# Local attention's probabilities turned in 32x32 squares and put together in DRAM

## The chip, the cores and the metric

The kernel runs on one core of one Trainium2 chip. The metric is the device time of one execution in microseconds (us), the median of several runs. Four engines compute: TensorE (PE in the profile; its weight loads are PEld), VectorE (DVE), ScalarE (ACT) and GpSimd (POOL). SyncE (SP) issues the DMAs, one after the other from one queue. Each engine works through its instructions in the order in which they were written out, and waits where an operand isn't ready.

## The reference

The program is one layer of a decoder over 1024 tokens of width 1024, in float32. It has three branches (sparse attention, a convolution module, cross-attention to 256 memory tokens), which are merged by gates, and then a gated feed-forward network. The change lies in the sparse attention, which has 8 query heads in 2 groups of 4; the heads of a group share keys and values of width 64. Three kinds of attention are summed with a gate for each:

```
s_c = q . kc   -> p_c = softmax over the compressed blocks that have ended    -> o_c = p_c vc
s_s = q . ks   -> p_s = softmax over selected blocks of 64 keys, up to t      -> o_s = p_s vs
s_w = q . kw   -> p_w = softmax over the last 512 keys (local window)         -> o_w = p_w vw
o   = gate0 * o_c + gate1 * o_s + gate2 * o_w
```

With 1024 tokens there are 16 selectable blocks and 16 are taken, so "selected" is ordinary causal attention here. The local branch is causal attention over a window of 512 keys.

## The kernel before

Every matrix product keeps nearly full float32 accuracy by splitting operands into a high part (rounded to the type that PE multiplies fast) and the low remainder. The helper `split` (lines 130 to 132) does it: ScalarE writes the high part, VectorE (or GpSimd) the difference. All products go through `mm` (line 146), so most PE rows carry line 146.

**The attention's order of work.** The loop at lines 822 to 836 runs over 8 tiles of 128 query rows (`i`), 2 groups (`g`), and within a group over four units `(br, hp)`: the causal branch (`br` 1) for head pairs 0 and 1, and then the local branch (`br` 2) for head pairs 0 and 1. That makes 64 units. For a unit `scores` is written down; `values` of the same unit is written down `LAG` units later, just ahead of that later unit's `scores`. The compressed branch (`br` 0) has its scores in the first 64 columns of the causal branch's first product, and one `values` call for all four heads of a group.

**`scores`** (lines 726 to 777). At the first unit of a group the four heads' queries are scaled, turned by PE (line 735) and split. For each head the products of queries (high and low) with keys go into a PSUM bank of pool 0, up to 512 columns at a time. VectorE adds the mask and takes the running maximum in one instruction (line 769, written to `tiles`), ScalarE takes the exponential and its sum (line 773). `softmax_tail` (lines 691 to 699) takes the reciprocal of the sums on VectorE and scales the probabilities by reciprocal and gate on GpSimd. The probabilities stand with 128 query rows on the partitions and keys along the columns; the tile that holds two heads comes from the pool `slabs` or the pool `wsp` (`wslab`, 3 buffers), two and three times in five.

**`values`** (lines 779 to 820). To multiply with the values, the probabilities must have the keys on the partitions. For two key blocks and two heads at a time PE turns four 128x128 squares into one PSUM bank of pool 1 (line 803), `split` makes the two parts from there into a `t4` tile, and PE multiplies them with the stored values. The stationary operand holds the values' high and low parts side by side (64 columns each), so a block takes two products of 256 columns (two heads x 128 queries), one for each part of the probabilities. All three branches of a group add up in one bank `OB` (pool 2, one bank); the compressed branch starts it and the local branch's last product ends it. Then ScalarE and VectorE add the bank's two halves (lines 814 and 817), and SP stores the result to `od` in DRAM (line 820).

**Work that fills PE's gaps.** The products of the three merge gates (lines 839 to 860) are independent of the attention. They have the lowest priority; their weights come by DMA into `fst` and are split into the `fsl` tiles, they have one bank of their own (`pf`), ScalarE copies the result out (line 859) and SP stores it to `zd` (line 860). Beyond the first 12 of 24 column blocks, each may start only behind one of the attention's `anchors`, a list of (weight, instruction) pairs that `values` appends, so that they spread over the attention.

**What sets the order.** The program text gives each instruction a priority; a planner then simulates the engines and writes out one fixed order for each engine and for SP's queue, taking the first instruction in priority that its model believes ready, and hands out the buffers of each pool as they come free. `follow` adds an order between two instructions of one engine without a semaphore. PSUM has 8 banks: `cnt` (line 60) gives 3, 3 and 1 to pools 0, 1 and 2, and the last is `pf`'s. The same pools serve the later stages through `bank` and `anybank`; the last stage takes its eight banks by the list `pools` (line 1177).

## Time and profile before

| | |
|---|---|
| median of 3 runs | 1700.61 us (1700.05 to 1700.92) |
| the profiled execution | 1701.01 us, span 1699.3 us |
| PE busy | 1675.7 us (99%) |
| VectorE busy | 1074.8 us (63%) |
| ScalarE busy | 732.9 us (43%) |
| GpSimd busy | 517.7 us (30%) |
| moved by DMA | 211.81 MB |
| the attention's stretch | about 453 to 840 us of the span |

Times in the profile are us from the start of the span unless marked ns. A group row gives line, engine, operation, tiles (out<-in), shapes, count, then the busy time in us and the mean duration of one in ns, and the engine's idle time just ahead of it with what ended it. The busy time of a group counts overlapping matmuls once, so it is less than count times mean. A row of a timeline gives start, length and the merged run of instructions. Line numbers are the kernel's; a helper's line stands for all that call it.

### The profile page before, as it was taken

The page shows a single profiled execution, that of the slowest core. Times are in us where ns is not written, and L with a number is a line of the kernel's source. Part 1 is how long each engine was busy: PE and PEld are TensorE (multiplying, and loading weights), DVE is VectorE, ACT ScalarE, POOL GpSimd, SP SyncE. Part 2 cuts the span into 40 slices and gives each one's busy share as a digit, 9 for nine tenths or more (in the row PEclk, how much of TensorE's full clock was granted, in tenths as well). Part 3 has the DMA queues.
Part 4 walks back from the last instruction along what each step waited for, and adds up shares of the span by engine and source line. Part 5 has one row for each costly group of instructions (what it writes and reads, how often), then busy time and mean ns, then how long its engine had stood idle before and what let it go on. Part 6 is the DMA issues. An engine that isn't in the chain of part 4 may idle for free.

```text
span 1699.3 us, 23161 instructions
## 1 busy us (share of the span) xinstructions
PE 1675.7 (99%) x8424; PEld 1415.4 (83%) x8424; DVE 1074.8 (63%) x1890; ACT 732.9 (43%) x1376; POOL 517.7 (30%) x478
## 2 busy tenths in 40 slices
PE   7999999999999999999999999999999999999999
PEld 6887898888888889989888888788888888888887
DVE  6278888688446677777766626756445455466655
ACT  6311444342356667666655424433222222233332
POOL 0000002120145544534105501465656776310000
PEclk9999999999999999999999999999999999999999
DMA  8012444221122111111674323133233545793773
GB/s 282 34 40 87 140 135 129 99 94 63 50 76 69 51 51 38 48 38 48 225 252 137 113 86 121 64 119 118 88 112 114 167 147 170 280 392 129 230 231 124
DMA packets 176728, 211.81 MB, mean 125 GB/s; under 512 B 11284, under 2 KB 113988, under 8 KB 175590
## 3 DMA queue, kind: packets, MB, share of 16 engines
q1 hardware_dynamic: 176614, 210.34, 37.3%
q8 instruction: 66, 1.08, 0.3%
q14 instruction: 48, 0.39, 0.1%
HBM read 155.77 MB, written 54.53 MB: 124 GB/s over the span
## 4 chain that ended last, share of the span: by engine, by line
PE 93%; DVE 3%; DMA 2%; ACT 1%; issue 1%; POOL 0%; SPq 0%; ACTq 0%; DVEq 0%; POOLq 0%
PE ps L146 56%; PE pf L146 19%; PE ps L1251 11%; PE ps L803 3%; PE pf L1251 1%; DVE slab L132 1%; DMA slab<-in_x_dram 1%; DVE t L132 1%; PE ps L233 1%; DMA slab<-in_mem_dram 0%; PE ps L603 0%; PE ps L735 0%; PE ps L787 0%; DMA st<-in_w_in_dram 0%; ACT t L131 0%
## 5 line engine op out<-in xcount | busy, mean ns | idle before, releaser
L146 PE MATMUL ps<-slab,wsl 128*128 128x512 f32 (+1 forms) x1652 | 367.9, 381 | 1.9 <-DVE sm L140 0.8
L146 PEld LDWEIGHTS ps<-slab,wsl 128*128 128x128 f32 x1652 | 300.0, 188 | 63.4 <-issue 1.9
L146 PE MATMUL pf<-slab,fsl 128*128 128x512 f32 x1236 | 322.1, 399 | 1.5 <-ACT fz L859 1.5
L146 PEld LDWEIGHTS pf<-slab,fsl 128*128 128x128 f32 x1236 | 223.6, 188 | 43.5 <-ACT fz L859 2.6
L1147 DVE TENSOR_TENSOR t<-ps,t 128x512 f32<-128x512 f32 x130 | 88.8, 688 | 106.0 <-PE ps L146 104.6
L421 DVE SCALAR_TENSOR_TENSOR slab<-slab,cw 128x1023 f32<-128x1023 f32 (+14 forms) x120 | 152.2, 1268 | 2.1
L146 PE MATMUL ps<-slab,fsl 128*128 128x512 f32 x636 | 149.0, 391 | 1.6 <-DVE slab L132 1.6
L146 PEld LDWEIGHTS ps<-slab,fsl 128*128 128x128 f32 x636 | 119.2, 188 | 27.6 <-DVE slab L132 2.0
L146 PE MATMUL ps<-wsl,slab 128*128 128x512 f32 (+1 forms) x648 | 140.0, 360 | 0.1
L132 DVE TENSOR_TENSOR t<-ps,t 128x512 fp32r<-128x512 f32 (+2 forms) x192 | 117.8, 630 | 28.5 <-ACT t L131 27.2
L146 PE MATMUL ps<-t,slab 128*128 128x256 f32 (+1 forms) x672 | 127.7, 299 | 0.7 <-DVE t L132 0.7
L146 PEld LDWEIGHTS ps<-wsl,slab 128*128 128x128 f32 x648 | 108.1, 189 | 17.3 <-DVE slab L225 0.3
L146 PE MATMUL ps<-slab,slab 128*128 128x512 f32 x480 | 117.5, 396 | 1.3 <-ACT slab L224 0.9
L1251 PE MATMUL ps<-wsl 128*128 128x512 f32 x495 | 118.7, 389 | 0.0
L131 ACT CAST t<-ps 128x512 fp32r<-128x512 f32 (+2 forms) x192 | 98.9, 539 | 43.7 <-PE ps L803 20.0
L593 POOL TENSOR_SCALAR t<-t,sm 128x256 f32<-128x256 f32 x32 | 25.6, 816 | 291.2 <-DVE sm L589 261.5
L146 PEld LDWEIGHTS ps<-t,slab 128*128 128x128 f32 x672 | 102.9, 189 | 8.2 <-DVE t L132 1.2
L1251 PEld LDWEIGHTS ps<-wsl 128*128 128x128 f32 x495 | 92.9, 188 | 19.3
L146 PEld LDWEIGHTS ps<-slab,slab 128*128 128x128 f32 x480 | 90.8, 191 | 21.2 <-ACT slab L224 1.7
L131 ACT CAST wsl<-st 128x1024 fp32r<-128x1024 f32 x59 | 62.0, 1051 | 79.3 <-PE ps L146 42.4
L146 PE MATMUL ps<-slab,qt 128*128 128x384 f32 (+6 forms) x400 | 96.0, 337 | 0.0
L132 DVE TENSOR_TENSOR wsl<-st,wsl 128x1024 fp32r<-128x1024 f32 x58 | 74.6, 1287 | 31.9 <-ACT wsl L131 31.7
(249 smaller groups left out, 2722.3 us busy)
## 6 DMA issues: line engine op xcount, KB each, us to landing
t<-in_w_down_dram SPq DMA_DIRECT2D x70, 256.0 KB, 4.0
fst<-in_w_in_dram SPq DMA_DIRECT2D x24, 512.0 KB, 3.7
zd<-fz SPq DMA_DIRECT2D x48, 256.0 KB, 2.0
t<-zd SPq DMA_DIRECT2D x24, 512.0 KB, 4.4
st<-in_w_gate_dram SPq DMA_DIRECT2D x22, 512.0 KB, 4.1
st<-in_w_up_dram SPq DMA_DIRECT2D x22, 512.0 KB, 4.2
ad<-t SPq DMA_DIRECT2D x44, 256.0 KB, 2.6
st<-in_w_in_dram SPq DMA_DIRECT2D x20, 512.0 KB, 3.7
```

The costliest lines, as they stand in the source:

```text
L131: m = nc.scalar.copy(hi, src)
L132: return m, (eng or nc.vector).tensor_tensor(lo, src, hi.bitcast(F32), op=OP.subtract)
L146: m = nc.tensor.matmul(o, a, b, start=start, stop=stop)
L233: m = nc.tensor.transpose(b[:, kk, tt * P:(tt + 1) * P], js[tt][:, k * P:(k + 1) * P], ident)
L421: return nc.vector.scalar_tensor_tensor(acc[:, s:], u[:, :S - s], cw[:, ct, 30 - s:31 - s], acc[:, s:], op0=OP.mult, op1=OP.add)
L593: nc.gpsimd.tensor_scalar(pm[:, tt, h, :], pm[:, tt, h, :], rec[:, j:j + 1], 1.0, op0=OP.mult, op1=OP.mult)
L803: nc.tensor.transpose(b[:, j - j0, h, :], tiles[h][:, j * P:(j + 1) * P], ident)
L1147: nc.vector.tensor_tensor(o, a_, b_, op=OP.add)
L1251: nc.tensor.matmul(B[t], a_, b_, start=start and k == 0 and j == 0, stop=k == FH - 1 and j == 2, skip_group_check=True)
```

## The change

The local branch's probabilities are no longer turned by PE.

- VectorE turns each 32x32 square of them in place of PE (`turn_window`): for two heads at a time, so that the tile `T_` has, in each quarter of 32 partitions, a 32-key part of each of its columns' blocks on the partitions, and head and 32 queries along the columns. It is issued one unit later, behind the next unit's last maximum (`behind`). A fifth key block goes to the free end of the first head pair's tile.
- After the second head pair, SP stores each of the four quarters of partitions (`a`, 32 queries each) to a new DRAM tensor `wd`, by one DMA for up to four blocks and one for the fifth: pieces of 512 bytes. In `wd` the squares lie so that key blocks of 128 can be read with keys on the partitions and all four heads' queries along 512 columns.
- `window_values` loads two key blocks at a time from `wd` (512 KB), splits them in SBUF into `t4` tiles, and multiplies: two products of 512 columns (four heads) for a block. It runs in two parts, in the places of the two head pairs' `values`.
- The order within a group is turned round: the local branch's two units come first, then the causal branch's two. The local branch starts the bank `OB`, the causal branch ends it. There are two such banks (pool 2), and pool 1 has two in place of three; the last stage's list is changed to match. `LAG` is 6 in place of 4.
- The probabilities of the causal branch always come from `slabs`, those of the local branch from `wslab`; the counter `turn[0]`, which later stages use to alternate buffers, is no longer advanced in `scores`.
- One reciprocal instead of two serves the causal and compressed branches of a pair.

```diff
-WB, LAG, SPREAD = 6, 4, 97
+WB, LAG, SPREAD = 6, 6, 97
...
-    cnt = [3, 3, 1]
+    cnt = [3, 2, 2]
...
-        turn[0] += 1
-        pt = (wslab if turn[0] % 5 < 3 else slab)([2, S], F32)
-        tiles = [pt[:, h, :nb * P] for h in range(2)]
-        mn_, den = small(8), small(4)
+        if br == 1:
+            short = PC[(i, g)]
+            pt = slab([2, S], F32)
+            tiles = [pt[:, h, :nb * P] for h in range(2)]
+        else:
+            pt = wslab([2 * S], F32)
+            tiles = [pt[:, h * nb * P:(h + 1) * nb * P] for h in range(2)]
+        mn_, den, rec = small(8), small(4), small(4)
...
+        n = 4 if br == 1 else 2
+        nc.vector.reciprocal(rec[:, :n], den[:, :n])
...
+        for f_ in behind:
+            f_(peak.ins)
+        behind.clear()
+        if br == 2:
+            behind.append(lambda after: turn_window(i, g, hp, nb, pt, after))
         return tiles
+
+    def turn_window(i, g, hp, nb, pt, after):
+        full = min(nb, 4)
+        if hp == 0:
+            WT[(i, g)] = [(wslab([16, 4, 32], F32)[:, :4 * full], 0, full)]
+            if nb > 4:
+                t5 = pt[:, 2 * nb * P:2 * nb * P + 512].rearrange("p (n h q) -> p n h q", h=4, q=32)
+                WT[(i, g)].append((t5, 4, 1))
+        both = pt[:, :2 * nb * P].rearrange("p (h n k) -> p n h k", h=2, k=32)
+        for T_, j0, n in WT[(i, g)]:
+            follow(nc.vector.transpose(T_[:, :, 2 * hp:2 * hp + 2, :], both[:, 4 * j0:4 * (j0 + n)]), after,
+                   "turned behind the next maxima")
+        if hp == 1:
+            for T_, j0, n in WT[(i, g)]:
+                for a in range(4):
+                    nc.sync.dma_start(
+                        wd[2 * i + g, 4 * j0:4 * (j0 + n), :, a, :].rearrange("n k q -> k n q"),
+                        T_[32 * a:32 * a + 32].rearrange("p n h q -> p n (h q)"))
+
+    def window_values(i, g, part):
+        k0 = max(0, i - 4)
+        nb = i + 1 - k0
+        if part == 0:
+            OB[(i, g)] = bank([4, P], at=2)
+        o = OB[(i, g)].rearrange("p h (a q) -> p h a q", a=4)
+        pairs = list(range(0, nb, 2))
+        cut = (len(pairs) + 1) // 2
+        for j0 in (pairs[:cut] if part == 0 else pairs[cut:]):
+            n = min(2, nb - j0)
+            lo, hi = t4([2, 4, 4, 32], F32R), t4([2, 4, 4, 32], F32R)
+            nc.sync.dma_start(lo[:, :n].bitcast(F32).rearrange("p j a h q -> p j (a h q)"),
+                              wd[2 * i + g, 4 * j0:4 * (j0 + n)].rearrange("(j b) k a q -> (b k) j (a q)", b=4))
+            split(hi[:, :n], lo[:, :n], lo[:, :n].bitcast(F32))
+            for j in range(n):
+                for hl, t_ in enumerate((hi, lo)):
+                    m = mm(o, VSW[1][:, k0 + j0 + j, g, :], t_[:, j].rearrange("p a h q -> p h a q"),
+                           j0 == 0 and j == 0 and hl == 0, False)
+        if part == 0 or len(pairs) > 1:
+            anchors.append((WB + nb, m.ins))
...
-            for br, hp in ((1, 0), (1, 1), (2, 0), (2, 1)):
+            for br, hp in ((2, 0), (2, 1), (1, 0), (1, 1)):
...
-    pools = ([0, 0, 0, 2], [1, 1, 1, None])
+    pools = ([0, 0, 0, 2], [1, 1, 2, None])
```

More of the change, by code (lines that the diff above doesn't have):

```diff
@@ L689, in balanced, with softmax_tail @@
         return [n] if n <= 4 else [n - n // 2, n // 2]
-    def softmax_tail(i, g, br, h0, den, tiles):
-        n = len(tiles)
-        rec = small(n)
-        nc.vector.reciprocal(rec, den)
-        if br == 0 and i == 0:
-            nc.vector.tensor_scalar(rec, rec, rowok, None, op0=OP.mult)
-        for h in range(n):
+    def softmax_tail(i, g, br, h0, rec, tiles):
+        for h in range(2):
             c0 = (4 * g + h0 + h) * 3 + br
             nc.gpsimd.tensor_scalar(tiles[h], tiles[h], rec[:, h:h + 1], gsb[:, i, c0:c0 + 1], op0=OP.mult, op1=OP.mult)
-    QS, OB, QN, PC, anchors = {}, {}, {}, {}, []
+    QS, OB, QN, PC, WT, anchors, behind = {}, {}, {}, {}, {}, [], []
+    wd = drp.tile([2 * NT, 20, 32, 4, P], F32, tag="wd", name="wd")
     def load_q(i):
@@ L726, in scores @@
     def scores(i, g, br, hp):
-        if br == 1 and hp == 0:
+        if br == 2 and hp == 0:
             if g == 0 and i + 1 < NT:
@@ L768, in scores @@
                 acc = mn_[:, 3 * h + ci:3 * h + ci + 1]
-                nc.vector.tensor_tensor_reduce(tiles[h][:, o:o + n * P], b[:, lead:], m, op0=OP.add, op1=OP.min,
-                                               scale=-0.125, scalar=BIG if last is None else last, accum_out=acc)
+                peak = nc.vector.tensor_tensor_reduce(
+                    tiles[h][:, o:o + n * P], b[:, lead:], m, op0=OP.add, op1=OP.min, scale=-0.125,
+                    scalar=BIG if last is None else last, accum_out=acc)
                 last = acc
@@ L773, in scores @@
             nc.scalar.activation(tiles[h], tiles[h], AF.Exp, scale=-1.0, bias=last, accum_out=den[:, h:h + 1])
+        n = 4 if br == 1 else 2
+        nc.vector.reciprocal(rec[:, :n], den[:, :n])
         if br == 1:
-            softmax_tail(i, g, 0, 2 * hp, den[:, 2:4], short[2 * hp:2 * hp + 2])
-        softmax_tail(i, g, br, 2 * hp, den[:, 0:2], tiles)
-        return tiles
+            if i == 0:
+                nc.vector.tensor_scalar(rec[:, 2:4], rec[:, 2:4], rowok, None, op0=OP.mult)
+            softmax_tail(i, g, 0, 2 * hp, rec[:, 2:4], short[2 * hp:2 * hp + 2])
@@ new lines, in scores @@
+        softmax_tail(i, g, br, 2 * hp, rec[:, 0:2], tiles)
+        for f_ in behind:
[3 more added lines that the diff above has]
+            behind.append(lambda after: turn_window(i, g, hp, nb, pt, after))
+        return tiles
+    def turn_window(i, g, hp, nb, pt, after):
[15 more added lines that the diff above has]
+                        T_[32 * a:32 * a + 32].rearrange("p n h q -> p n (h q)"))
@@ L779, in values @@
     def values(u, tiles):
         i, g, br, hp = u
-        if br == 0:
-            OB[0] = bank([4, P], at=2)
-        o = OB[0]
+        if br == 2:
+            window_values(i, g, hp)
+            return
+        o = OB[(i, g)]
         if br == 0:
@@ L789, in values @@
             split(pt[:64], pt[64:], b[:64])
[L790 removed]
+            m = mm(o.rearrange("p h q -> p (h q)"), vcmp[:, g, :], pt.rearrange("p h q -> p (h q)"), False, False)
             anchors.append((3, m.ins))
             return
[L793 to L795 removed]
+        nb = i + 1
         oh = o[:, 2 * hp:2 * hp + 2, :].rearrange("p h q -> p (h q)")
@@ L808, in values @@
                 for hl in range(2):
-                    m = mm(oh, V[:, k0 + j, g, :], pt[:, hl, j - j0, :], False,
-                           br == 2 and hp == 1 and j == nb - 1 and hl == 1)
+                    m = mm(oh, VSW[0][:, j, g, :], pt[:, hl, j - j0, :], False,
+                           hp == 1 and j == nb - 1 and hl == 1)
         anchors.append((WB + nb, m.ins))
-        if br == 2 and hp == 1:
+        if hp == 1:
             bot = t2([2, 2, P], p=64)
```

7 lines of the change are left out of this document (2 added, 5 removed).

## The prediction

> **What bounds the kernel now.** I read the busy shares first, then the chain that ended last, then the stretch of the attention alone.
>
> ```profile
> PE 1675.7 (99%) x8424; PEld 1415.4 (83%) x8424; DVE 1074.8 (63%) x1890; ACT 732.9 (43%) x1376; POOL 517.7 (30%) x478
> PE 93%; DVE 3%; DMA 2%; ACT 1%; issue 1%; POOL 0%; SPq 0%; ACTq 0%; DVEq 0%; POOLq 0%
> PE ps L146 56%; PE pf L146 19%; PE ps L1251 11%; PE ps L803 3%; PE pf L1251 1%; DVE slab L132 1%; DMA slab<-in_x_dram 1%; DVE t L132 1%; PE ps L233 1%; DMA slab<-in_mem_dram 0%; PE ps L603 0%; PE ps L735 0%; PE ps L787 0%; DMA st<-in_w_in_dram 0%; ACT t L131 0%
> ```
>
> TensorE (PE) is the bound: busy 99%, and 93% of the chain. L803, the turning of probabilities that the change attacks, is 3% of the chain. So an instruction taken from PE is worth its own time, as long as nothing else comes to bind. Whether it does is read from the attention's own stretch, split where the work changes: tiles 0 to 3, tiles 4 to 7, and the end.
>
> ```profile
> core 0: us, PE busy (x) PEld busy (x) DVE busy (x) ACT busy (x) POOL busy (x), PEclk, DMA share, GB/s
> 453.00:596.00 143.00, 139.04 (x806) 119.86 (x805) 78.84 (x322) 90.54 (x268) 69.92 (x103) 1.00 0.22 67
> 596.00:811.00 215.00, 212.86 (x1378) 193.30 (x1377) 156.34 (x515) 147.13 (x338) 98.90 (x112) 1.00 0.14 44
> 811.00:840.00 29.00, 28.15 (x174) 24.84 (x173) 22.61 (x39) 17.40 (x30) 3.47 (x4) 1.00 0.64 227
> 645.00:670.00 25.00, 25.00 (x164) 22.96 (x163) 19.37 (x65) 18.07 (x44) 12.99 (x14) 1.00 0.16 48
> 860.00:880.00 20.00, 20.00 (x87) 16.18 (x87) 16.95 (x21) 13.10 (x13) 0.00 (x0) 1.00 0.74 254
> ```
>
> The columns: length, then busy us of PE, weight loads, VectorE (DVE), ScalarE (ACT), GpSimd (POOL), the granted clock, DMA share. The attention is 387 us (453 to 840); PE is idle for 6.9 us of it, at full clock. DVE is at 55% for tiles 0 to 3 and at 73% (179.0 of 244) after; in the fullest group, 645 to 670, at 77%. The last row is later work: there DVE reached 85% with PE never idle, the highest such share I found.
>
> **The change part by part. PE's work.** The local branch has 1, 2, 3, 4, 5, 5, 5, 5 key blocks for the eight row tiles, 30 in all. With two groups and four heads that is 240 turned squares, and with two groups, two head pairs and two halves of each value, 240 products of 256 columns. The squares go; 120 products of 512 columns take the place of the 240. PE's prices come from unbroken runs, since single durations overlap:
>
> ```profile
> 695.24 2.90 PE L146 MATMUL pf<-slab,fsl 128*128 128x512 f32 x12
> 699.91 1.12 PE L146 MATMUL ps<-t,slab 128*128 128x256 f32 x8
> 700.86 0.60 PE L803 MATMUL ps<-identr,wsl 128*128 128x128 f32 x4
> L803 PE MATMUL ps<-identr,wsl 128*128 128x128 f32 x312 | 49.6, 272 | 0.0
> L146 PE MATMUL ps<-t,slab 128*128 128x256 f32 x528 | 100.6, 293 | 0.7 <-DVE t L132 0.7
> L146 PE MATMUL pf<-slab,fsl 128*128 128x512 f32 x709 | 190.5, 402 | 0.5 <-ACT fz L859 0.5
> ```
>
> The three last rows give one instruction's mean (272, 293 and 402 ns). A run of n takes one mean and n-1 steps: a square steps at (0.60-0.272)/3 = 0.109 us, 256 columns at (1.12-0.293)/7 = 0.118, 512 columns at (2.90-0.402)/11 = 0.227. Off: 240 x 0.109 = 26.2. Products: 240 x 0.118 - 120 x 0.227 = 28.3 - 27.2 = 1.1. PE loses 27.3 us, 9.1 in tiles 0 to 3 (10 of 30 blocks) and 18.2 after. The chain agrees roughly (3% of 1699 over 528 squares is 0.097 each). PE being the bound, 27 us is the most to be won, save a few of the 6.9 us of idle time.
>
> **DVE's work.** No row shows a transpose on DVE. For each head pair it turns 256 columns per block: one instruction of 256 to 1024, and for a fifth block a second of 256.
>
> ```profile
> L873 DVE TENSOR_TENSOR slab<-slab,slab 128x1024 f32<-128x1024 f32 x3 | 3.7, 1225 | 1.3 <-DMA slab<-ud 1.3
> L132 DVE TENSOR_TENSOR t<-ps,t 128x512 fp32r<-128x512 f32 x112 | 75.6, 687 | 14.1 <-ACT t L131 13.4
> L132 DVE TENSOR_TENSOR t<-ps,t 128x256 fp32r<-128x256 f32 x40 | 16.5, 418 | 0.9 <-ACT t L131 0.7
> L694 DVE RECIPROCAL sm<-sm 128x2 f32<-128x2 f32 x96 | 15.6, 163 | 26.9 <-ACT slab L773 11.2 <-ACT wsl L773 10.0 <-ACT t L760 4.9
> L214 DVE TENSOR_SCALAR slab<-slab,sm 128x1024 f32<-128x1024 f32 x10 | 7.5, 753 | 0.3
> L132 DVE TENSOR_TENSOR wsl<-t,wsl x42: 1209/1224/2193, 1104.9 to 1683.2; 128x1024 fp32r<-128x1024 f32 x42
> ```
>
> I take the ordinary two-input price at each width: 0.42, 0.69, 0.95 (between its neighbours) and 1.225 us for 256 to 1024. Per pair that is 0.42, 0.69, 0.95, 1.225 for tiles 0 to 3 and 1.645 for each later one; times four, 39.4 us in 48 instructions, 26.3 of them from tile 4 on. Bounds for 1024 columns: 0.753 (a one-input row) and 2.193 (the slowest two-input one), so 24 to 71 us. I take the middle row, being the plain pass over fp32 that most of the rows show.
>
> The Trainium skill, "VectorE: DVE Perf Modes", section on the three transpose paths, gives 311 ns on VectorE for 128x128 bf16 and 390 on TensorE, a small gain for VectorE. By it an estimate for 240 squares, one by one, is 75 us on DVE; the trace's own 0.109 us step for TensorE is far below the page's 390, so its order of the two does not hold for this kernel, and no run so far shows the other.
>
> DVE saves elsewhere. The splits into two parts were 48 of 512 columns and 24 of 256 (43.0 us); they become 24 of 1024 and 12 of 512, from memory (37.6): 5.4 saved, 3.6 from tile 4 on. Reciprocals go from 96 to 64: 5.2, half of it late. Net on DVE +28.8, late +20.1. From tile 4 on DVE has 199.1 us where PE needs 244 - 18.2 = 225.8: 88%; in the fullest group 96% (21.9 of 22.7). That is where the gain leaks. At the shown 85% the late part lasts 199.1/0.85 = 234.2, a loss of 8.4; the bounds are none, and 33 us if 77% is all DVE reaches (258.6). I take 8.4.
>
> ```profile
> L131 ACT CAST t<-ps 128x512 fp32r<-128x512 f32 x112 | 63.9, 583 | 16.6 <-PE ps L803 16.1
> L131 ACT CAST t<-ps 128x256 fp32r<-128x256 f32 x40 | 14.6, 370 | 4.2 <-PE ps L803 3.9
> L131 ACT CAST wsl<-st 128x1024 fp32r<-128x1024 f32 x2 | 2.1, 1052 | 6.2 <-DMA st<-in_w_mem_out_dram 6.2
> L773 ACT ACTIVATE slab<-slab,sm 128x640 f32<-128x640 f32 x20 | 16.6, 832 | 10.9 <-DVE sm L769 10.8
> ```
>
> ACT's casts go from 48 x 0.583 + 24 x 0.370 = 36.9 us to 24 x 1.052 + 12 x 0.6 = 32; ACT is at 67% late (164.5 of 244), so this is worth nothing on the path. POOL's scalings stay. The compressed branch's reciprocal now waits for the long exponentials; the six units before its use cover that, and uncovered it is one 0.83 us exponential in each of 32 pairs, 27 us.
>
> **The way through DRAM.** Each group of four heads stores 256 KB per block, in four or eight DMAs from 32 partitions each, and loads it back 512 KB at a time: 96 stores and 36 loads on SP's queue.
>
> ```profile
> fst<-in_w_in_dram SPq DMA_DIRECT2D x24, 512.0 KB, 3.7
> zd<-fz SPq DMA_DIRECT2D x48, 256.0 KB, 2.0
> 811.00 0.37 SPq L820 DMA_DIRECT2D od<-t  x1
> DVE t L561 <- DMA t<-qraw: 2.7, 3, 1.3
> SPq L860 <- ACT fz L859: 219.5, 29, 15.7
> ```
>
> From the last transpose to a usable operand: eight issues at 0.37 (3.0), a store landing (2.0), an issue and a load (4.1), a cast (1.05) and a subtraction (1.2), 11.3 us. A group of four units lasts 25 us late; some three units lie between the second pair's transpose and the first product at LAG 6, so about 19 us of cover, and 15 in the early tiles, where there are four issues fewer. Traffic grows by 31 MB over about 370 us, 85 GB/s on top of 44 to 67: the engines stay under half. Queued behind a load that waits for its stores are the gate product's store (L860), its next weights and the next queries; SP already stands 219.5 us before L860, so order alone is cheap here. What is left is that a load is later than the plan thought. Loads that fed DVE directly did this for 2.7 us in 8 (0.34 each); 36 such are 12 us on ACT, of which, with gate products in between, I charge a quarter to PE: 3. Bounds 0 and 12.
>
> **Banks, lag, order.** The second output bank frees PE from one evacuation per group (0.58 + 2 x 0.42 = 1.4 us, now covered by products); the transposes that remain have two banks in place of three.
>
> ```profile
> L814 ACT COPY t<-ps 64x512 f32<-64x512 f32 x16 | 9.3, 584 | 6.4 <-PE ps L146 6.2
> L817 DVE TENSOR_TENSOR t<-ps,t 64x256 f32<-64x256 f32 x32 | 13.3, 416 | 4.8 <-ACT t L814 4.4
> PE ps L146 <- DVE t L132: 3.8, 6, 1.4
> 817.50 3.86 DMA st<-md
> 826.06 3.41 DMA st<-in_w_mem_out_dram
> ```
>
> A wait on DVE cost PE 0.63 us, six times. One for every group is 10 us at worst, none at best; I charge 1. Six units in flight leave two more to drain and hold all four free slabs to the end, so the next stage's operands may come later; the two loads shown already stand on the chain there. Charged at nothing, since the drain itself (six units of turning and products) and the last gate products give PE work meanwhile; up to 7 us (both loads again) if they don't. Buffer rotation after the attention shifts by 64 turns: nothing, as PE there has its operands ahead.
>
> **Sum.** -27.3 + 8.4 + 3 + 1 = -15. The profiled execution took 1701.0 us (span 1699.3); the median of the runs is 0.4 below. 1701.0 - 15 - 0.4 = 1685.6; I forecast 1685.
>
> **The rivals.** *All of it.* DVE keeps up as PE needs: 1700.6 - 27.3 = 1673. For it: PE was full with DVE at 85%. Against: in-order DVE at 96% in the fullest group leaves no room for a chain of maxima, exponential and reciprocal.
>
> *DVE becomes the bound.* If a transpose costs the dear bound (1.79 times my price), late DVE is 199.1 + 0.79 x 26.3 = 220 us, 97% of PE's need; at 85% it lasts 259, 15 longer than now; less 9 won in the early tiles, 1706. The same comes of my price with DVE stuck at 77%. By the Trainium skill's 311 ns per square it would end here too.
>
> *The round trip comes late (slower than before).* PE works in order; if the plan places a part's first product where it believes the load done, each of the 28 parts (one per group for tiles 0 and 1, two later) stands x us. From x = 27.3/28 = 1.0 us nothing is won. The loads on the chain were waited for up to 3.9 us; with 1.6 us, between the 0.34 and that, 28 x 1.6 - 27.3 = +17: 1718. For it: eight issues and two landings in line; against: 15 to 19 us of cover.
>
> The Trainium skill, "SBUF — State Buffer", section "Door 1", says that 32 partitions reach 8 of the 16 DMA ports and gives 189 GB/s for them against 328 for all. By it each store is longer by an estimated 0.6 us, four in line 2.4; it speaks for this rival, and no row here has a 32-partition store to test it.
>
> **How the numbers follow.** Partial gain, 1676 to 1695: 0.41. All of it: 0.20. No difference (gain eaten by waits): 0.10. DVE the bound: 0.12. Late round trip: 0.17. A difference under 0.2% (3.4 us) is not told from none. So faster 0.61, same 0.10, slower 0.29. The range goes from 1668 (all, with 5 us of PE's idle time) to 1714, which leaves out the worse half of the late round trip; the forecast's own is 1676 to 1695.
>
> **What would show it.** Right: 288 squares left on L803's successor; 120 products of 512 columns; DVE transposes near 1.2 us for 1024 columns; the attention about 15 us shorter with DVE near 85% late and PE idle by 10 to 15 us, released by DVE. Wrong: transposes at 2 us and PE waiting on DVE all through (DVE bound), or PE waiting for the low half's cast behind a load from the new DRAM tensor (late round trip). If PE's idle time stays at 7 us, the gain is all of it; if the stretch after 840 changes by over 4 us, I missed something outside the attention.

## The result, and the profile after

The changed kernel takes 1718.05 us (median of 4 runs, 1713.56 to 1720.76) beside 1700.76 us for the kernel before: 1.0098 times as long, 95% interval 1.0076 to 1.0121. I had forecast 1685, and my range ended at 1714. The profiled execution took 1718.12 us, its span is 1716.4 us. The line of busy shares and the first line of the chain, from the page of the changed kernel:

```profile
PE 1671.2 (97%) x8064; PEld 1390.8 (81%) x8064; DVE 1108.5 (65%) x1870; ACT 734.3 (43%) x1342; POOL 520.3 (30%) x478
PE 63%; DVE 7%; DMA 5%; ACT 4%; issue 3%; POOL 2%; SPq 1%; DVEq 0%; ACTq 0%; POOLq 0%
```

PE has 360 matmuls less (8424 before) and is "busy" for only 4.5 us less, though by the table below its work is 27.2 us less: the busy time hides what is lost. The chain says it more plainly: PE's share fell from 93% to 63%, and VectorE, DMA, ScalarE and waiting to issue took its place. The groups that the change touches, by form, in the attention (452 to 870 us) of the changed kernel:

```profile
L852 PE MATMUL ps<-identr,slab 128*128 128x128 f32 x288 | 45.8, 273 | 0.0
L146 PE MATMUL ps<-t,slab 128*128 128x512 f32 x120 | 44.3, 457 | 16.4 <-DVE t L132 8.9 <-ACT t L131 7.4
L799 DVE STREAM_TRANSPOSE wsl<-wsl 128x1024 f32<-128x1024 f32 x20 | 24.8, 1240 | 0.3 <-POOL wsl L694 0.3
L799 DVE STREAM_TRANSPOSE wsl<-wsl 128x256 f32<-128x256 f32 x20 | 8.2, 410 | 1.8 <-POOL wsl L694 1.8
L799 DVE STREAM_TRANSPOSE wsl<-wsl 128x768 f32<-128x768 f32 x4 | 3.9, 970 | 0.0
L799 DVE STREAM_TRANSPOSE wsl<-wsl 128x512 f32<-128x512 f32 x4 | 2.8, 706 | 0.2 <-POOL wsl L694 0.2
L132 DVE TENSOR_TENSOR t<-t,t 128x1024 fp32r<-128x1024 f32 x24 | 34.6, 1443 | 15.4 <-ACT t L131 15.2
L132 DVE TENSOR_TENSOR t<-t,t 128x512 fp32r<-128x512 f32 x12 | 8.4, 698 | 9.1 <-ACT t L131 9.0
L131 ACT CAST t<-t 128x1024 fp32r<-128x1024 f32 x24 | 25.1, 1046 | 17.6 <-DMA t<-wd 16.0 <-DVE t L866 1.5
L131 ACT CAST t<-t 128x512 fp32r<-128x512 f32 x12 | 7.4, 618 | 20.0 <-DMA t<-wd 18.7 <-PE ps L146 1.3
```

The counts are as announced: 288 squares on PE, 120 products of 512 columns, 48 transposes on VectorE, which take 24.8 + 8.2 + 3.9 + 2.8 = 39.7 us. New is what stands in the last column: the products waited 16.4 us for loaded pairs, the casts 34.7 us (16.0 + 18.7) for the loads from the new DRAM tensor. The same stretches as before, and two more (length, busy us of PE, weight loads, VectorE, ScalarE, GpSimd, clock, DMA share, GB/s):

```profile
453.00:596.00 143.00, 135.11 (x712) 112.05 (x712) 94.95 (x331) 92.38 (x267) 74.46 (x109) 0.99 0.45 132
596.00:811.00 215.00, 201.95 (x1102) 170.72 (x1100) 172.91 (x499) 142.81 (x306) 101.57 (x106) 0.98 0.49 144
645.00:670.00 25.00, 22.55 (x107) 18.85 (x106) 18.28 (x55) 15.66 (x35) 12.44 (x12) 0.86 0.48 135
1060.00:1105.00 45.00, 39.48 (x182) 32.52 (x181) 28.81 (x37) 24.75 (x42) 14.84 (x9) 0.96 0.22 77
```

VectorE reaches 80% from 596 to 811 us (172.9 of 215), not 85%, and PE idles for 20.9 us in the first two rows (6.1 before). The clock, 1.00 all through before, falls to 0.86 in a group, and PE idles again long after the attention.

**Where the time went.** I priced each matmul of a trace at its step (0.109 us for 128 columns, 0.118 for 256, 0.227 for 512, other widths between) and took the sum from the length of a stretch. What is left is the time in which PE was not at its step, be it idle, slowed or at half clock. In us, for the executions profiled (the runs below the second row are the experiments):

| kernel | PE's work | lost to 452 | 452 to 870 | 870 to 1140 | after 1140 |
|---|---|---|---|---|---|
| before | 1653.6 | 20.3 | 18.2 | 4.0 | 3.2 |
| changed | 1626.4 | 21.0 | 50.0 | 15.8 | 3.2 |
| b1_order | 1653.6 | 20.8 | 24.3 | 13.8 | 3.1 |
| c1_banks | 1653.6 | 20.8 | 38.2 | 9.5 | 3.2 |
| c3_order | 1653.6 | 19.9 | 11.6 | 4.0 | 3.3 |
| a3_no_turning2 | 1626.4 | 20.5 | 33.2 | 13.8 | 3.1 |
| d3_phase | 1626.4 | 20.8 | 50.9 | 8.6 | 3.1 |
| g1_t4_phase | 1626.4 | 20.1 | 52.0 | 6.3 | 3.2 |
| g2_all_noturn | 1626.4 | 19.9 | 43.0 | 3.1 | 7.6 |

PE's work fell by 27.2 us. Lost are 31.8 us more in the attention and 11.8 more in the stage after it: 27.2 were won, 44.3 lost.

The loss has three parts: PE stands idle, or it runs at half clock (the last section), or it works, but slower than its step. From 452 to 870 us PE is idle for 7.0 us before and 22.2 in the changed kernel, and half clock costs 0 and 6.8. What remains, the slow part, is 11.2 us before and 21.0 in the changed kernel. In the five kernels with three turning banks (before, and c2_lag, c3_order, c4_after331 and d2_232 below) this part is 9.6 to 13.5 us, and in the fifteen with two it is 17.5 to 23.9. So it goes with that bank.

### The profile page after: what moved, and what is told of

Read it like the earlier page. It is cut to its first block, busy times and chain, and to the rows that moved or that the text cites. A ratio compares the mean times of both kernels' runs of the same rounds, so it can differ in the third digit from the quotient of the medians.

```text
span 1716.4 us, 22544 instructions
## 1 busy us (share of the span) xinstructions
PE 1671.2 (97%) x8064; PEld 1390.8 (81%) x8064; DVE 1108.5 (65%) x1870; ACT 734.3 (43%) x1342; POOL 520.3 (30%) x478
## 4 chain that ended last, share of the span: by engine, by line
PE 63%; DVE 7%; DMA 5%; ACT 4%; issue 3%; POOL 2%; SPq 1%; DVEq 0%; ACTq 0%; POOLq 0%
PE ps L146 36%; PE pf L146 13%; PE ps L1300 11%; DVE t L132 2%; DMA t<-wd 2%; DMA t<-zd 1%; PE pf L1300 1%; POOL slab L988 1%; PE ps L852 1%; DVE slab L132 1%; ACT slab L131 1%; DVE wsl L799 1%; DMA wd<-wsl 1%; DVE slab L770 1%; ACT t L131 1%
## 5 line engine op out<-in xcount | busy, mean ns | idle before, releaser
L146 PE MATMUL ps<-slab,wsl 128*128 128x512 f32 (+1 forms) x1580 | 351.9, 381 | 0.0
L146 PEld LDWEIGHTS ps<-slab,wsl 128*128 128x128 f32 x1580 | 286.9, 188 | 58.3 <-issue 1.2
L146 PEld LDWEIGHTS pf<-slab,fsl 128*128 128x128 f32 x1260 | 231.4, 189 | 50.2 <-ACT fz L908 3.2
L146 PE MATMUL ps<-slab,fsl 128*128 128x512 f32 x708 | 165.9, 390 | 0.0
L146 PEld LDWEIGHTS ps<-slab,fsl 128*128 128x128 f32 x708 | 132.8, 188 | 27.7
L421 DVE SCALAR_TENSOR_TENSOR slab<-slab,cw 128x1021 f32<-128x1021 f32 (+15 forms) x120 | 151.5, 1265 | 1.9
L146 PE MATMUL ps<-wsl,slab 128*128 128x512 f32 (+1 forms) x690 | 148.8, 363 | 1.8 <-ACT slab L131 1.8
L146 PE MATMUL ps<-t,slab 128*128 128x256 f32 (+1 forms) x552 | 129.0, 336 | 18.6 <-DVE t L132 11.2
L146 PEld LDWEIGHTS ps<-wsl,slab 128*128 128x128 f32 x690 | 115.7, 189 | 20.9 <-ACT slab L131 2.3
L146 PEld LDWEIGHTS ps<-t,slab 128*128 128x128 f32 x552 | 90.7, 193 | 39.3 <-DVE t L132 20.0
L132 DVE TENSOR_TENSOR wsl<-st,wsl 128x1024 fp32r<-128x1024 f32 x58 | 77.0, 1330 | 33.4 <-ACT wsl L131 33.2
L131 ACT CAST wsl<-st 128x1024 fp32r<-128x1024 f32 x58 | 60.8, 1049 | 71.5 <-PE ps L146 33.7
L132 DVE TENSOR_TENSOR t<-ps,t 128x512 fp32r<-128x512 f32 (+2 forms) x120 | 77.1, 648 | 13.3 <-ACT t L131 12.1
L131 ACT CAST t<-ps 128x512 fp32r<-128x512 f32 (+2 forms) x120 | 65.1, 555 | 43.3 <-PE ps L852 23.5
```

The source lines that it names most:

```text
L131: m = nc.scalar.copy(hi, src)
L132: return m, (eng or nc.vector).tensor_tensor(lo, src, hi.bitcast(F32), op=OP.subtract)
L146: m = nc.tensor.matmul(o, a, b, start=start, stop=stop)
L421: return nc.vector.scalar_tensor_tensor(acc[:, s:], u[:, :S - s], cw[:, ct, 30 - s:31 - s], acc[:, s:], op0=OP.mult, op1=OP.add)
```

## The experiments

Three theories stood at the start: that the loaded pairs come late (L, later D and T: for the stores, for the buffers), that VectorE's added work holds the attention up (V), and that the small parts, order, lag and banks, cost more than I thought (O, later B for the banks, G for the lag, Q for the order), with the buffers' rotation (R) and a place in the later order (S) for the loss behind the attention. The runs that tell most come first.

**The changed kernel's three small parts, alone in the kernel before.** b1_order has the turned order of units (the local branch opens the output bank, the causal one closes it), LAG 6 and the banks 3, 2, 2 with the last stage's list, and no other part of the change.

```diff
-WB, LAG, SPREAD = 6, 4, 97
+WB, LAG, SPREAD = 6, 6, 97
...
-    cnt = [3, 3, 1]
+    cnt = [3, 2, 2]
...
-            for br, hp in ((1, 0), (1, 1), (2, 0), (2, 1)):
+            for br, hp in ((2, 0), (2, 1), (1, 0), (1, 1)):
```

> The kernel before with the change's order and banks alone: local units first in a group, six units in flight, two output banks and two banks for turned squares; TensorE turns everything as before. If order, lag or banks cost something by themselves (theory O): 1705 or more. If the loss comes from the way through DRAM or from VectorE (theories L, V): 1701 within 3.

1716.13 us, ratio 1.0092 [1.0075, 1.0109]: 15.6 us lost without turning anything on VectorE, by the step that I had charged at 1 us. That is its price in the kernel before, where PE still turns all the squares; c4_after331 and d3_phase below show parts of it in the changed kernel. The three parts one by one, each in the kernel before; first the banks, with the last stage's list (`[1, 1, 2, None]`):

```diff
-    cnt = [3, 3, 1]
+    cnt = [3, 2, 2]
```

> The kernel before with one edit: pool 1 has two PSUM banks and pool 2 two (cnt [3, 2, 2], and the last stage's list to match); order of the units, LAG and the turning on TensorE are as before. The order of units, LAG 6 and the banks together cost 15.6 us. Theory B (the banks): pool 1's third bank was what let TensorE run ahead of the two-part split; with two, TensorE waits for the split of L132 in the attention, and in the stages after it too: 1708 to 1716, and the first product of the stage after the gates (before 1121.5 us) comes at least 5 us later. Theory O (order and LAG): two banks are enough for the turning, and the extra bank of pool 2 helps: 1698 to 1703, with that landmark within 2 us.

```diff
-WB, LAG, SPREAD = 6, 4, 97
+WB, LAG, SPREAD = 6, 6, 97
```

> The kernel before with LAG 6 in place of 4 and nothing else. Theory G (the lag): with six units in flight instead of four the slabs run short, the last group drains longer (38.8 us from the last but one store of the attention's result to the last in the run with all three edits, 29.2 before) and the next stage's loads come later: 1706 to 1712, all of it in the attention and at its end. Theory B: within 3 us of before, 1698 to 1704.

```diff
-            for br, hp in ((1, 0), (1, 1), (2, 0), (2, 1)):
+            for br, hp in ((2, 0), (2, 1), (1, 0), (1, 1)):
```

> The kernel before with only the order within a group turned round (the local branch's two units first, the causal ones last; the local branch opens the output bank, the causal one closes it); LAG 4 and the banks 3, 3 and 1 as before. Theory Q (the order): the attention then ends on the longest unit (8 key blocks and not 5), whose turning and products have only gate work beside them, and the next stage starts later: 1704 to 1710, with the first products of the memory branch (before 841.7 us) 5 to 10 us later and nothing lost behind that. Theories B and G: 1698 to 1703.

Banks: 1726.59 us, 1.0152 [1.0136, 1.0167], 26.2 lost, more than either theory had. Lag: 1700.37, 1.0006 [0.9996, 1.0016], nothing; theory G falls. Order: 1693.80, 0.9963 [0.9950, 0.9976], 6.6 us **won**, the opposite of theory Q. That is the fastest kernel of the study and beats both. In the table it loses 6.6 us less than before in the attention, 5.0 of them idle time (7.0 to 2.0 us); the kernel before has idle times of 1.4 to 1.7 us ahead of compressed products and of the turning of queries, and here none is over 1 us. What else the other order does isn't shown. The sum of the three, 19.6, is more than the 15.6 together. PE's longest waits in the attention of c1_banks; the first has no row in the kernel before, the second had 3.8 us there:

```profile
PE ps L803 <- DVE t L132: 7.0, 9, 1.7
PE ps L146 <- DVE t L132: 4.3, 7, 1.7
```

L803 is the turning of squares into pool 1: it waits for the subtraction that reads the bank, nine times. The rows name 11.3 us. The table has 20.0 us more lost in the attention than before (38.2 - 18.2): 8.5 of idle time, 5.1 of half clock and 6.4 in which PE is slower than its step.

**Another division of the eight banks for the changed kernel.**

```diff
-    cnt = [3, 2, 2]
+    cnt = [3, 3, 1]      # c4_after331
+    cnt = [2, 3, 2]      # d2_232
```

> The changed kernel with the banks of before: three in pool 1 and one in pool 2 (cnt [3, 3, 1], and the last stage's list as before), so that a group's local products wait for the evacuation of the group before. LAG, order and the turning on VectorE stay. Theory B: it wins back what the third bank was worth, above all outside the attention: 1702 to 1711. Against it (the second output bank is needed for the products of the local branch to run ahead): 1720 to 1735. Theory O: within 3 us of the changed kernel, 1715 to 1721.

> The changed kernel with three banks in pool 1 again, taken from the scores: cnt [2, 3, 2] (the last stage's list to match). Theory B (pool 1's third bank is what was lost): 1700 to 1710. Rival, scores: with two banks the products of queries and keys can't run ahead of VectorE's maxima, which is where VectorE is late already: 1722 to 1740. Not told apart from no effect between 1714 and 1721.

1735.78 us, 1.0205 [1.0190, 1.0220], and 1784.71 us, 1.0490 [1.0473, 1.0508] (one of the latter's four executions took 9148 us, which stays unexplained; the ratio leaves it out). Both are worse than the changed kernel: theory B, as a remedy, falls twice. PE's rows show which bank is missed. With one output bank (c4_after331) PE waits for the evacuation (L866):

```profile
PE ps L146 <- DVE t L866: 10.0, 4, 6.5
```

and with two score banks (d2_232) the loaded pairs are later still:

```profile
PE ps L146 <- ACT t L131: 37.4, 13, 4.7
```

The third turning bank is missed in the changed kernel too: with it back (c4_after331) the slow part of the loss falls from 21.0 to 12.0 us and the loss from 870 to 1140 us from 15.8 to 10.4, but idle time and half clock in the attention rise from 29.0 to 58.9, the wait for the evacuation among it. So the change wants three turning banks, two output banks and three score banks, with one more for the gates: nine, and there are eight. c4_after331 shows something else. In all runs with 3, 3, 1 the stores of the stage after the gates (`hd`) take 38.4 us from the first to the last; in those with 3, 2, 2, 16 slabs and nothing moved there some 46 to 47. The rows of before, of the changed kernel, and of c4_after331 (count, duration, first and last start):

```profile
L1093 SPq DMA_DIRECT2D hd<-slab x4: 327/332/339, 1022.1 to 1060.5; - x4
```

```profile
L1142 SPq DMA_DIRECT2D hd<-slab x4: 327/332/338, 1030.6 to 1077.9; - x4
```

```profile
L1142 SPq DMA_DIRECT2D hd<-slab x4: 326/333/339, 1051.4 to 1089.8; - x4
```

**What that is.** The timeline of the changed kernel in that stage:

```profile
1058.13 0.33 SPq L1142 DMA_DIRECT2D hd<-slab  x1
1058.94 1.84 SPq L1128 DMA_DIRECT2D t<-in_x_dram  x1
1059.23 1.52 PE L146 MATMUL ps<-wsl,slab 128*128 128x512 f32 x6
1060.59 0.60 PE L233 MATMUL ps<-identr,t 128*128 128x128 f32 x4
1061.70 0.69 DVE L1135 TENSOR_TENSOR slab<-ps,t 128x512 f32<-128x512 f32 x1 [3.60 <-DMA t<-in_x_dram]
1064.86 2.82 PE L233 MATMUL ps<-identr,t 128*128 128x128 f32 x12 [3.67 <-DVE t L1052]
1070.65 1.52 PE L146 MATMUL ps<-fsl,slab 128*128 128x512 f32 x6
```

and of the kernel before:

```profile
1050.38 0.33 SPq L1079 DMA_DIRECT2D t<-in_x_dram  x1
1052.33 1.64 PE L146 MATMUL ps<-wsl,slab 128*128 128x512 f32 x6
1053.81 1.53 PE L146 MATMUL ps<-fsl,slab 128*128 128x512 f32 x6
1056.67 1.54 PE L146 MATMUL ps<-fsl,slab 128*128 128x512 f32 x6
1058.05 1.47 PE L233 MATMUL ps<-identr,t 128*128 128x128 f32 x12
```

The rows of a tile are turned (L233, 12 squares) once their load, addition and norm are through. Before, products of the stage's last tile (24 matmuls in the order as written) stand ahead of them on PE and cover that chain: the squares follow without a gap. In the changed order the same products stand behind the squares (from 1070.65): PE has nothing to do for 3.67 us. Whether the planner finds a free bank for that product at the right moment depends on the pools' sizes and on where the list that deals out pools has got to. I moved that list's counter:

```diff
+    turn[1] += 4
     H = [None] * 4
```

> The changed kernel with the counter that deals out pools to the turned pairs moved on by 4 ahead of the stage after the gates (from turn[1] to turn[1] + 4); nothing else. In TensorE's order this puts the last product of that stage (24 matmuls) ahead of the last 12 transposes that wait for rows, as in the kernel before, and no longer behind them. Theory S: the loss after the attention is this place in the order, with the half clock behind the wait; the stage from its first to its last store takes 38 to 40 us as before (47.3 in the changed kernel), and the time is 1706 to 1712. Rival: two banks are too few there in any order: 1715 to 1721, stage 44 us or more.

1712.74 us, 1.0073 [1.0056, 1.0090], 5.3 less than the changed kernel, and the stage is back to 38.5 us:

```profile
L1143 SPq DMA_DIRECT2D hd<-slab x4: 326/333/339, 1031.5 to 1070.0; - x4
```

The median is just above the 1712 I gave, but the mechanism is as theory S has it: the place in the order, not the number of banks as such. Of the 11.8 us that the table has more from 870 to 1140 us, 7.2 are gone (15.8 to 8.6); the other 4.6 stay open. It isn't the counter that the change itself left alone (`turn[0]`):

```diff
         nb = i + 1 - (0 if br == 1 else max(0, i - 4))
+        turn[0] += 1
```

> The changed kernel with the buffer counter advanced by one in each unit's scores again, as before the change, so that the stages after the attention take the same buffers as before. Theory R (the 8 us that are lost between 1040 and 1105 us come from the shifted rotation): 1710, and the stretch from the first merged product to the first feed-forward product as long as before the change. Theory P (that loss comes from the planner's order after another attention, or from its end): within 3 us of 1718, the loss still there.

1716.21 us, 1.0081 [1.0053, 1.0109], with the late stage still long: theory R falls, and that part of the prediction (nothing) was right.

**VectorE's added work.** Each transpose is cut to 32 columns (one square in each quarter of the partitions); what is stored is a fixed tile, made once (`stay`; its lines are left out below).

```diff
-            follow(nc.vector.transpose(T_[:, :, 2 * hp:2 * hp + 2, :], both[:, 4 * j0:4 * (j0 + n)]), after,
+            follow(nc.vector.transpose(T_[:, 0, 2 * hp, :], both[:, 4 * j0, 0, :]), after,
...
```

> The changed kernel with VectorE's turning cut to one 32x32 square for each instruction (a fixed tile is stored in its place, so the local branch's values are left out of the result); stores, loads, casts and products as they were. VectorE loses about 35 us of work. Theory V (VectorE's added work binds): 1718 becomes 1693 or less. Theory L (late loads): stores start at most 1.6 us earlier, the casts wait as before, and it stays above 1708.

1699.72 us, 0.9998 [0.9989, 1.0007]: 18.3 us less than the changed kernel, 16.8 of it in the attention by the table. What is left of the transposes:

```profile
L800 DVE STREAM_TRANSPOSE wsl<-wsl 128x32 f32<-128x32 f32 x48 | 9.9, 207 | 0.9 <-POOL wsl L694 0.3
```

So VectorE is rid of 29.8 of the 39.7 us. Its transposes do cost what I feared, and about twice what I had put down. (The cut also frees the first pair's tile sooner, since no fifth block is stored from its end; no run separates that.) Yet even so the kernel only equals the one before, with 27 us less work on PE.

**The way through DRAM.** The loads take an older tensor of the same size instead of the one just stored:

```diff
-                              wd[2 * i + g, 4 * j0:4 * (j0 + n)].rearrange("(j b) k a q -> (b k) j (a q)", b=4))
+                              qraw[0, 0:n].rearrange("j p c -> p j c"))
```

> The changed kernel, except that the operands of the local branch are loaded from an older DRAM tensor (the unscaled queries, written before the attention), by loads of the same size and number. The stores into the new DRAM tensor stay, but nothing waits for them; the local branch's values are left out of the result. Theory D (the round trip comes late): ScalarE's casts wait 34.7 us for these loads in the changed kernel, TensorE 19.1 us for the parts made from them, and three pieces of half clock in the attention take 6.8 us; without the wait for the stores most of that goes: 1696 to 1706. Theory V (VectorE's added work alone): the loads are late because VectorE turns late, and the rest of the path is no shorter with the loads early: 1712 to 1720.

1720.48 us, 1.0119 [1.0104, 1.0134]: no gain at all. Theory D falls in so far as it blames the wait for the stores to land: SyncE stood 14.7 us for that in the changed kernel, and without it ScalarE's casts still wait 29.1 us (34.7 in the changed kernel). The waits of d1_ready in the attention, ScalarE's and SyncE's:

```profile
ACT t L131 <- DMA t<-qraw: 29.1, 16, 6.0
SPq L819 <- DVE t L132: 24.8, 10, 5.4
SPq L819 <- PE ps L146: 19.6, 18, 2.8
```

SyncE holds the loads for 44 us until an earlier pair's buffer is free (VectorE's subtraction, PE's products). But the run leaves something as it was: SyncE works in order, and the loads still stand behind their group's stores, which wait for VectorE's transposes. A group of d1_ready:

```profile
641.41 6.06 SPq L804 DMA_DIRECT2D wd<-wsl  x8
648.06 0.94 SPq L819 DMA_DIRECT2D t<-qraw  x2
```

The eight stores are issued as the transposes end (641.7), and take 6.06 us; the loads follow 0.6 us later, as in the changed kernel. In 15 of the 16 groups the first load stands behind the last store, in 7 of them by 0.1 us. So d1_ready doesn't refute that the way through DRAM is late; it shows that the place in the queue and the buffers make a load late, and not the wait for the landing. With both cuts together:

> The two cuts together: the loads from the older tensor, and VectorE's transposes cut to one 32x32 square per instruction and quarter of partitions, with a fixed tile stored; the local branch's values are left out of the result. The transposes' cut alone gave 1699.7 (18 less than the changed kernel). If late loads and VectorE's work are separate losses, 1680 to 1690; if they are one loss, seen twice, 1695 to 1701. What is then left above 1690.8 (before, less TensorE's 27 us, plus the late stage's 8 and bank waits of 9) would belong to neither.

1700.27 us, 0.9997 [0.9987, 1.0006], the same as the transposes' cut alone. (The 1690.8 in that expectation is 1700.8 - 27 + 17.) Then the buffers, with a control, since two more `t4` buffers had to be paid for with a slab:

```diff
-    t4p = ctx.enter_context(tc.tile_pool(name="t4p", bufs=4))
+    t4p = ctx.enter_context(tc.tile_pool(name="t4p", bufs=6))      # e1_t4 alone
-N_MAIN, N_W, N_F = 16, 3, 2
+N_MAIN, N_W, N_F = 15, 3, 2                                         # e1_t4 and e2_15
```

> The changed kernel with six buffers instead of four in the pool of the loaded pairs (t4), paid for with one of the 16 slabs (15). To be read against the run with 15 slabs alone. Theory T (buffers): SyncE stands 37.7 us in the attention before loads whose buffer isn't free (21.9 until VectorE's subtraction, 15.8 until TensorE's products), so two more buffers start the loads earlier and ScalarE's casts wait less than 20 us for them (34.7 in the changed kernel): 6 to 11 us faster than its control. Theory V (VectorE's work is late, whatever the loads do): within 3 us of its control.

> The changed kernel with 15 slabs in place of 16 and nothing else: the control of the run with six buffers for loaded pairs. If the slabs are not short: 1714 to 1721; if they are: 1722 to 1735.

1712.35 us, 1.0069 [1.0054, 1.0084], and the control 1725.69, 1.0154 [1.0137, 1.0171]: the missing slab costs 7.6 us, so slabs are short. The buffers are worth 13.3 us (10.4 between the two executions profiled), yet theory T is not shown by it: in the attention ScalarE's casts of e1_t4 still wait

```profile
ACT t L131 <- DMA t<-wd: 30.1, 18, 5.8
```

and the time lost there fell by only 2.5 us (57.5 to 55.0); from 870 to 1140 us it fell by 7.3 (13.8 to 6.5). So what the buffers gain is mostly behind the attention, where the same pool serves the stages that follow; which of them gains isn't shown.

**Moving work within the path.** ScalarE's casts put behind the last exponential, so that no exponential stands behind a cast that waits for its load:

```diff
-            split(hi[:, :n], lo[:, :n], lo[:, :n].bitcast(F32))
+            c_, _ = split(hi[:, :n], lo[:, :n], lo[:, :n].bitcast(F32))
+            follow(c_, exps[-1], "cast behind the last exponential")
...
```

> The changed kernel with one order added: ScalarE's cast of a loaded pair of blocks stands behind the last exponential written down before it, and not wherever the planner believes the load done. Theory L (loads land later than planned, ScalarE stands at the cast, VectorE and TensorE behind it, and TensorE's clock drops after): ScalarE's 35 us of waiting for these loads falls under 10, TensorE's idle time in the attention from 22 us to under 12, the clock back to 1.00 there, and 1718 becomes 1700 or less. Theory V (VectorE's added work binds): within 3 us of the changed kernel, the idle time stays, released by VectorE.

1748.71 us, 1.0285 [1.0270, 1.0301]: far worse, which neither theory had. ScalarE's wait for the loads does fall, from 34.7 to 13.9 us, but the pair comes later: PE's weight loads wait 32.1 us for low halves in the attention (21.2 in the changed kernel; these rows hold loaded and turned pairs together). A wait taken off ScalarE is not time won. And the pair's subtraction on GpSimd in place of VectorE:

```diff
-            split(hi[:, :n], lo[:, :n], lo[:, :n].bitcast(F32))
+            split(hi[:, :n], lo[:, :n], lo[:, :n].bitcast(F32), nc.gpsimd)
```

> The changed kernel with the subtraction of the loaded pairs on GpSimd and no longer on VectorE (36 subtractions, 42.0 us on VectorE in the changed kernel: 24 x 1.443 and 12 x some 0.6). Theory V: VectorE's added work is what costs the 18 us that the cut of the transposes gave back, so taking away as much of other work gives back the like: 1698 to 1709. Rival, latency: the pair is made later (a subtraction of 1024 columns takes GpSimd 2.4 to 2.5 us), TensorE waits for it, and the time is 1718 to 1730.

> The last one with the counter of the turned pairs moved on by 4 as well (which took 5.3 us off the changed kernel). Theory V: 1692 to 1704, which would be the change's gain net of a better place in the order. Rival, latency: 1712 to 1725. Either way 4 to 7 us below the run with GpSimd alone if the two losses are separate.

1726.49 us, 1.0152 [1.0137, 1.0167], and with the counter moved 1719.81, 1.0113 [1.0098, 1.0128]. VectorE is rid of 43.0 us, more than the 29.8 of the transposes' cut, and 8 us are lost, where that cut won 18. GpSimd's row:

```profile
L132 POOL TENSOR_TENSOR t<-t,t 128x1024 fp32r<-128x1024 f32 x24 | 57.2, 2389 | 28.0 <-ACT t L131 26.2 <-DMA t<-wd 1.4 <-DMA od<-t 0.2
```

Each pair is made 0.95 us later (2389 - 1443 ns), at the end of the chain. So the 18 us are not settled by the amount of VectorE's work alone: what lies on the chain from the scores to the loaded pair counts. The run doesn't separate this from a second effect, that GpSimd, which also scales the probabilities, gets so much more to do. The two losses do add up: the counter gave 6.7 us here, 5.3 above.

**Both remedies, with and without the transposes.** g1_t4_phase is e1_t4 with `turn[1] += 4`; g2_all_noturn has the transposes' cut as well.

> The changed kernel with both remedies that took something off it: six buffers for the loaded pairs (15 slabs) and the counter of the turned pairs moved on by 4 ahead of the stage after the gates. If the two gains are separate (5.8 and 5.3 us off the changed kernel): 1704 to 1709. If they are the same loss after the attention (the run with six buffers lost 6.5 us between 870 and 1140 us where the changed kernel loses 15.8): 1709 to 1713. In no case below the kernel before.

> The same with VectorE's transposes cut to one 32x32 square per instruction and quarter of partitions, and a fixed tile stored (the local branch's values are left out of the result). Theory V (the amount of VectorE's work is a loss of its own, 18 us): 14 to 20 us below the run with both remedies, 1686 to 1694. Rival (the transposes only lengthen waits that come from the loads and the buffers): less than 8 us below it.

1709.17 us, 1.0049 [1.0032, 1.0066]: the two remedies overlap, as the second theory has it (1709 to 1713). And 1698.77, 0.9984 [0.9973, 0.9994]: 10.4 less, between the two theories. The cut of the transposes is worth 18 us with the buffers as they are and 10 with both remedies. So the prices don't simply add up; that a part of this one is a wait shared with the loads would explain it, but isn't shown.

## Why the prediction was wrong

**PE's work: right.** -27.3 was the term, -27.2 the sum over the two traces.

**VectorE's work: the price of a transpose right, the rest not.** Predicted 39.4 us, measured 39.7; 1225 ns for 1024 columns against 1240, and 0.42, 0.69 and 0.95 against 0.41, 0.71 and 0.97. The split of the loaded pairs was to save 5.4 us on VectorE and saves nothing: 34.6 + 8.4 = 43.0, as before, since a subtraction took 1443 ns and not 1225. So VectorE has 33.7 us more (1108.5 - 1074.8) where I had 28.8. What I took from it, a loss of 8.4 us at 85%, is 18.3 in one pair of runs and 10.4 in the other. That the transposes cost time is right, its size was too small, and its dear bound (33) holds it. But the term divided VectorE's work by the highest share that it might reach. f1_pool, with 43 us less of that work and no gain, speaks against such a limit, and the chain shown below for one.

**The way through DRAM: the trip was priced about right, its cover was not there.** I charged 3 us (0 to 12). What neither the small parts (15.6) nor the transposes (18.3) explain is 17.3 - (15.6 + 18.3 - 27.2) = 10.6 us, by difference and not measured by itself; by the table it is 33.2 - 24.3 = 8.9 us in the attention. It also holds what no run took apart: the 9.9 us of transposes left in that cut, the new division of the tiles between `slabs` and `wslab`, and the joint reciprocal. In the group at 645 us of the changed kernel the chain can be read:

```profile
638.99 6.05 SPq L804 DMA_DIRECT2D wd<-wsl  x8
645.70 2.33 SPq L819 DMA_DIRECT2D t<-wd  x2
650.43 1.04 ACT L131 CAST t<-t 128x1024 fp32r<-128x1024 f32 x1 [3.23 <-DMA t<-wd]
651.38 0.82 ACT L775 ACTIVATE wsl<-wsl,sm 128x640 f32<-128x640 f32 x1
651.50 1.23 DVE L132 TENSOR_TENSOR t<-t,t 128x1024 fp32r<-128x1024 f32 x1 [4.25 <-ACT t L131]
651.52 0.80 PE L146 MATMUL ps<-t,slab 128*128 128x512 f32 x1 [1.99 <-ACT t L131]
```

The last transpose ends at 639.3 and the product starts at 651.5: 12.2 us, beside the 11.3 that I had added up, though the eight issues took 6.05 us and not 3.0. But PE had come to the product at 649.5, so the cover was 10.2 us and not the 15 to 19 of the prediction. In six of the 16 groups, all before 652 us, PE stood idle ahead of the first local product, 7.4 us in all; in the later groups the first pair came in time. ScalarE, in order, stands 3.23 us before the cast, the next exponential stands behind it, VectorE idles 4.25 us, PE 1.99. I had costed the cast as free since ScalarE is at 67%; a share of busy time says nothing on such a stall. The rival with the time 1718, "the round trip comes late", has this mechanism, but needs 28 x 1.6 = 44.8 us of it, and PE waited 16.4 for all loaded pairs. That it names the measured time is luck: the banks and the transposes make up the rest.

**Banks, lag, order: the step that failed.** "I charge 1" (none to 10) for the third turning bank, from six waits of 0.63 us, and for the lag and order nothing. In the kernel before they cost 15.6 us together, and one by one the banks 26.2, the lag 0, the order -6.6. A wait row of before prices a bank at the number of banks that there is; it does not say what happens with one less, when PE waits for the split (the rows of c1_banks) and falls behind its step. And I looked for the price in the attention only. "If the stretch after 840 changes by over 4 us, I missed something outside the attention": it changed by 11.8 (870 to 1140 us in the table). The same pools serve the stage after the gates, and the planner, with other pools, put a product behind the squares whose wait it had covered; moving it back gave 7.2 of the 11.8. That was a fault of looking, not of a price: the diff names `cnt`, and every `bank` call reads it.

**The sum.** -27.2 + 15.6 + 18.3 + 10.6 = +17.3, beside my -27.3 + 1 + 8.4 + 3. It closes by construction, since the last term is a difference, and the prices of the small parts and of the transposes come from two different kernels. The range ended at 1714, short of what my own bounds make together (33, 12, 10 and 7 on top of -27.3: 1735); three terms went past their likely value at once.

## What to carry to other kernels

A change that takes work from the bounding engine pays only what the buffers let it: count the PSUM banks that it needs against those that there are, and look at every later stage that shares the pools. Try the parts that look free (order, lag, bank counts) alone in the old kernel: here one of them cost more than the whole change, and another, the order of units, is worth 6.6 us and needs nothing else. For a trip through another memory, measure the cover (when does the waiting engine get there?) and not the trip alone. And judge a loss by the work an engine did in the time, not by its busy share.

## What the runs showed of the hardware

**PE's clock can halve behind an idle time of 2 us.** The trace of the changed kernel has five pieces at 0.50 between 452 and 1140 us, of 3.4 or 6.8 us (23.8 in all, so 11.9 us lost); the kernel before has none there. Three windows behind the chain just shown:

```profile
650.00:653.00 3.00, 1.01 (x2) 0.51 (x3) 1.50 (x3) 2.57 (x4) 0.09 (x1) 0.75 0.56 199
653.00:656.00 3.00, 3.00 (x9) 2.54 (x10) 2.96 (x10) 0.23 (x1) 3.00 (x3) 0.50 0.19 70
656.00:659.00 3.00, 3.00 (x10) 2.36 (x9) 2.14 (x4) 2.21 (x5) 0.89 (x1) 0.61 0.05 17
```

An idle time of 2.0 us ended at 651.5, and the half clock ran from 651.5 to 658.3: 3.4 us lost behind 2.0. Others followed idle times of 2.2, 3.7 and 1.4 us; one at 511.5 stands behind none over 1.3, and idle times of 1.6 us (at 540) and 1.8 us (at 978) were followed by none, so no single length decides. In c4_after331 the pieces in the attention cost 17.1 us, in c3_order none. The Trainium skill, "TensorE: Matmul & The Clock Gate", section "Part 1: The HAM clock gate", says that the gate goes to half rate after an idle window of about 3.4 us that runs freely. The pieces' length, 3.4 or twice that, agrees; that an idle time shorter than a window can be enough is seen here and does not follow from it. In this kernel a wait of 2 us on PE is thus to be priced at up to 5.4 (2.0 and 3.4).

**Stores from 32 partitions.** The 40 stores of 256 KB from 32 partitions took 3.7 us to land at the median in the attention of the changed kernel, those of the gates from 128 partitions 2.1 us beside them (2.0 before). I had taken 2.0; it did not decide, since d1_ready, without the wait for the landing, is no faster. Their issue was dearer too: the 96 stores to `wd` held SyncE for 61.8 us, 0.64 each, where I had taken 0.37.
